# VectorE's written order over more of the input projection and over memory attention, and the residual added by accumulating stores

## The chip, the cores and the metric

The kernel runs on one core of a Trainium2 chip. The metric is the device time of one execution in microseconds: 2166.34 us before, the median of three runs (2165.52 to 2167.77). The profiled execution took 2162.43 us.

The engines are called as in the profile: PE (TensorE, matmul), DVE (VectorE), ACT (ScalarE), POOL (GpSimd) and SP (SyncE, which here only issues DMAs).

## The reference

One residual block of a streaming encoder: 512 tokens, model width 2048, float32.

```
h = rms_norm(x, norm_g)
proj = h @ w_in                      # all branches and gates in one projection
c_gate, b_gate, u, conv_z, c_q, c_kv, k_rope_raw, mla_z, mem_q, mem_z, g_conv, g_mla, g_mem = split(proj)
o_conv = (b_gate * conv3(c_gate * u) * silu(conv_z)) @ w_conv_out
o_mla  = (latent_attention(c_q, c_kv, k_rope_raw) * silu(mla_z)) @ w_mla_out      # 16 heads, chunk-causal
o_mem  = (memory_attention(mem_q, mem) * silu(mem_z)) @ w_mem_out                 # 4 heads of 256 into 256 memory tokens
merged = sigmoid(g_conv) * o_conv + sigmoid(g_mla) * o_mla + sigmoid(g_mem) * o_mem
out = x + merged @ w_o
```

Memory attention normalizes queries and keys, takes softmax over the 256 memory tokens and multiplies by the values.

## The kernel before, in words

**Precision.** Each float32 product is three matmuls of high and low parts (mm3, L161 to L163): whi·xhi, whi·xlo, wlo·xhi. A weight tile is split by ACT, which copies the high part (L281, or L154 for plain tiles), and then by DVE, which subtracts it to get the low part (L282, or L155).

**Panels.** The input projection, the latent attention's output projection (mla_out) and w_o are done by panels of 2x2 blocks with seven products for eight (a Strassen form). Its weights are made by `pair_weights` (L270 to L283) in stages: a DMA into one of four raw buffers (L274, issued by SP), three sums on DVE (L276 to L278), the high part on ACT (L281), the low part on DVE (L282; two buffers each for whi and wlo). A panel has four chunks of 42 matmuls 128x256. After its last chunk the four banks are evicted and combined on DVE (L318 to L327) into a tile e.

**What hands out the stages.** `take()` gives the matmuls of chunk k their weights, and at that point emits whi and wlo of chunk k+1, the sums of k+2 and the load of k+3, and then pops one closure of the list `fills`. So the order of the calls of `take` is the order in which an engine sees these stages, if its order is as written. For PE and SP it always is. For DVE it is inside `tc.manual_schedule(engines={DVE})`; outside, a scheduler with its own estimate of times orders DVE's rows. ACT and POOL are ordered by the scheduler.

**The stages of the program, with their times in the profiled execution.** The memory's keys and values (0 to 106 us); the input projection (106 to 1354), whose first panels run while the transformed input xp is still being made; latent attention by heads, with the gates and memory queries (to 1646); memory attention (1646 to 1692) interleaved with conv_out; the rest of conv_out (to 1735); mla_out (to about 1900); mem_out (to 1984); w_o (1984 to 2156).

**Memory attention** is four generators, one a head, stepped by a string that is written by hand (0 to 3 is a head's next step, w a step of conv_out with three matmuls of 512 columns):

```
ORDER_MEM = "0 0 5w 1 1 5w 0 0 2 2w 1 1 3 2w 0 0 2 2 w 1 1 3 3 2w 2 2 2w 3 3 w 2 2 3 3"
```

The steps of a head (`mem_attend`) are: loads; two steps of scores, each for half of the queries (matmuls, max on DVE L1152, exponentials on ACT L1159, reciprocal of the sums on DVE L1162, scaling of p on ACT L1164); two steps of transposes of p on PE (L363) with the split of the transposed p into high and low parts, pt (ACT L130, DVE L132); two steps of values (matmuls, product with the gate on DVE L1180, split into my by ACT and DVE, store).

**w_o and the residual.** Each of its eight panels loads the residual xr (SP), adds the evicted e to it on DVE (L1350, two rows) and stores both halves by ACT. The last panel has its own tail. The inputs of w_o, xo0 to xo7, are made on the way from the merged branches by `pair_sums` and `pair_split` (`sums_out`, `split_out`).

Of the kernel before, what the change touches and what calls it, by code (L numbers as in the profile page):

```python
# [30 lines left out]
P = 128  # L31
# [76 lines left out]
def body(ctx, tc, a, out):  # L108
# [221 lines left out]
    def panels(xp, weight, n, make, finish, first="acc", tail=None):  # L330

        order = [(0, c) for c in range(3)] + [(1, c) for c in range(3)] + [(0, 3), (1, 3)]
        order += [(i, c) for i in range(2, n) for c in range(4)]
        upcoming(*[pair_job(weight[i][c]) for i, c in order])
        tags = (first, "aux" if first == "acc" else "acc")
        steps, es = {}, {}

        def go():  # L340
            for i, c in order:
                if c == 0:
                    es[i], middle = make(i)
# [179 lines left out]
    def staged_parts():  # L523
# [3 lines left out]
    upcoming(*plain_jobs([a["w_mem_kv"][grp][c] for grp in range(4) for c in range(8)], 512, True,  # L527
                         (staged_parts, None, None),
                         lambda c: memory_load(c + 1) if c < 4 else None))
    work = panels(xp, a["w_h"], len(SEQUENCE), lambda n: make(n), lambda n, e: finish(n, e), "aux")  # L530
    queue.insert(32 + 15, [lambda: rotary_weights()])
    parts_of_x = all_parts()
    manual_dve = ExitStack()
# [48 lines left out]
                nc.scalar.dma_start(mvdram[2 * (grp - 2) + i], t)  # L582
    for _ in parts_of_x:
        pass
    begin(2, 2)
    close_st()
    close_mt()
    pxb, close_xb = open_pool("xb", "right")
# [170 lines left out]

    conv_e = {}  # L760

    def make(n):
        return etile(), None

    angles = rotary()
# [50 lines left out]
    for i in (6, 7):  # L816
# [1 line left out]
        x_load(i, etile())  # L818
        steps = x_pair(i)
        fills += [lambda steps=steps: (next(steps), next(steps)), lambda steps=steps: next(steps)]  # L820
    for _ in range(6):
        next(work)
    manual_dve.close()
    for _ in work:
# [10 lines left out]

    PLACES = ((2, 3), (6, 7), (4, 5), (0, 1))

    def block(n):  # L840
        t = ph.tile([P, 2, S], F32R, tag=f"blk{n // 2}", name="blk", bufs=2)
# [289 lines left out]
    def mem_attend(head):  # L1131
# [9 lines left out]
        nc.sync.dma_start(z, mzdram[head])  # L1141
        yield
        pr = []
        for i2 in range(2):
            sb = bank("aux")
            for ii in range(2):
                cols = slice((2 * i2 + ii) * P, (2 * i2 + ii + 1) * P)
                for f in range(2):
                    mm3(sb[:, ii * M:(ii + 1) * M], (q[:, f, 0, cols], q[:, f, 1, cols]),
                        mk[f], f == 0, f == 1)  # L1150
            mx = pq.tile([P, 2], F32, tag="mx", name="mx", bufs=2)
            vec.tensor_reduce(out=mx, in_=sb.rearrange("p (a b) -> p a b", a=2), op=ALU.max, axis=AX.X)  # L1152
            nm = pq.tile([P, 2], F32, tag="nm", name="nm", bufs=2)
            c0 = 4 * head + 2 * i2
            vec.tensor_tensor(out=nm, in0=mx, in1=mqn[:, c0:c0 + 2], op=ALU.mult)
            sm = pq.tile([P, 2], F32, tag="sm", name="sm", bufs=2)
            p = pq.tile([P, 2, M], F32, tag="p", name="p", bufs=4)
            for ii in range(2):
                act.activation(p[:, ii], sb[:, ii * M:(ii + 1) * M], AF.Exp, scale=mqs[:, c0 + ii:c0 + ii + 1],  # L1159
                               bias=nm[:, ii:ii + 1], accum_out=sm[:, ii:ii + 1])  # L1160
            ri = pq.tile([P, 2], F32, tag="ri", name="ri", bufs=2)
            vec.reciprocal(ri, sm)  # L1162
            for ii in range(2):
                act.activation(p[:, ii], p[:, ii], AF.Copy, scale=ri[:, ii:ii + 1])  # L1164
                pr.append(p[:, ii])
            yield
        pts = []
        for j in range(2):
            b = transpose4([t[:, j * P:(j + 1) * P] for t in pr])
            t = pq.tile([P, 2, S], F32R, tag=f"pt{j}", name=f"pt{j}", bufs=2)  # L1170
            split(b, t[:, 0], t[:, 1])
            pts.append((t[:, 0], t[:, 1]))
            yield
# [12 lines left out]
    m = [mem_attend(head) for head in range(4)]  # L1186
    next(m[0])
    next(m[1])
    run(ORDER_MEM, w=conv, **{str(n): m[n] for n in range(4)})
    close_q()  # L1190
    close_g()
    close_q1()
# [99 lines left out]
    def split_out(n):  # L1292
# [8 lines left out]
                 17: ((split_out, 1), (merged, 2), (merged, 3), (gate_load, 5), (gate_load, 6)),  # L1301
                 22: ((sums_out, 2),), 23: ((split_out, 2),), 24: ((sums_out, 3),),
                 25: ((split_out, 3), (merged, 4), (merged, 5), (gate_load, 7)),
                 29: ((sums_out, 4),), 30: ((split_out, 4), (merged, 6)), 31: ((sums_out, 5),),
                 32: ((split_out, 5),)}

    late_blocks = []
    for k in (6, 7):
# [28 lines left out]

    def make_o(n):
        def middle():
            xrs[n] = pe.tile([P, 2, S], F32, tag="xr", name="xr", bufs=2)  # L1340
            nc.sync.dma_start(xrs[n].rearrange("p f n -> p (f n)"), a["xT"][:, n])
        return pe.tile([P, 8, H], F32, tag="e", name="e", bufs=2), middle

    def finish_o(n, e):
        fills.append(lambda: result(n, e))

    def result(n, e):
        xr = xrs[n]
        for f in range(2):
            vec.tensor_tensor(out=xr[:, f], in0=two(e)[:, f], in1=xr[:, f], op=ALU.add)  # L1350
            nc.scalar.dma_start(out[(2 * n + f) * P:(2 * n + f + 1) * P], xr[:, f])

    def tail_o(b, e):

# [10 lines left out]
        nc.sync.dma_start(out[15 * P:16 * P], xr[:, 1])  # L1365

    merged(7)
    fills += [lambda: None, lambda: sums_out(6), lambda: split_out(6), lambda: sums_out(7), lambda: split_out(7)]
    for n, _ in enumerate(work):
        if n == 8:  # L1370
            manual_dve.close()
# [79 lines left out]
```

## Time and profile before

| what | us |
|---|---|
| median of the runs | 2166.34 |
| profiled execution | 2162.43 |
| its span | 2160.7 |
| PE busy | 2122.6 (98% of the span) |
| DVE busy | 1728.2 (80%) |
| ACT busy | 1010.8 (47%) |

The span is the profiled execution from its first instruction to its last; the execution's own time is 1.7 us longer. A row of the chip's timeline has the start in us, the duration in us, the engine, the line and the operation with its output and inputs, and in brackets the idle time of the engine before it with what ended it. Rows on DVE and ACT overlap at their ends, so that the distance between two starts is a little less than a row's duration: a wlo of 128x1792 lasts 2.02 us, and the next row may start 1.94 after it.

### The profile page before, as it was taken

The numbers are of one execution on the slowest core, as the hardware profiler recorded it, in microseconds if no ns is written. First come the engines' busy times: TensorE is split into PE (matmuls) and PEld (weight loads), VectorE is DVE, ScalarE is ACT, GpSimd is POOL, SyncE is SP. The second block draws the span as 40 slices with busy tenths as digits, with TensorE's granted clock in tenths as the row PEclk, the third lists the DMA queues.
The fourth block names the chain that finished last, engine by engine and source line by source line (L and its number), as shares of the span: only waits on it lengthen the run. The fifth ranks groups of instructions, "written<-read, shape, count | busy, mean of one in ns | idle before, by whom it ended". The sixth has DMA issues, their size and how long they took to land.

```text
span 2160.7 us, 38707 instructions
## 1 busy us (share of the span) xinstructions
PE 2122.6 (98%) x16040; PEld 2037.7 (94%) x16040; DVE 1728.2 (80%) x2740; ACT 1010.8 (47%) x1235; POOL 130.9 (6%) x189
## 2 busy tenths in 40 slices
PE   9989999999999999999999999999999999999899
PEld 7889999999999999999999999898988899987899
DVE  5986878888888888888878876788886688856886
ACT  6743444444444344344444444777765533323333
POOL 0000000000000000000000000212111100011000
PEclk9999999999999999999999999999999999999999
DMA  8634443333333333343444336222346957667443
GB/s 330 248 98 137 158 135 128 128 127 128 127 127 127 125 125 126 126 136 133 137 137 142 131 129 241 90 104 81 112 158 245 355 203 208 201 213 199 141 162 107
DMA packets 93441, 338.51 MB, mean 157 GB/s; under 512 B 10896, under 2 KB 11152, under 8 KB 91216
## 3 DMA queue, kind: packets, MB, share of 16 engines
q1 hardware_dynamic: 70848, 252.58, 34.5%
q0 software_dynamic: 13920, 59.51, 8.6%
q10 hardware_dynamic: 8496, 23.94, 3.1%
q8 instruction: 125, 2.05, 0.4%
q14 instruction: 52, 0.43, 0.1%
HBM read 273.34 MB, written 62.65 MB: 156 GB/s over the span
## 4 chain that ended last, share of the span: by engine, by line
PE 84%; DVE 5%; ACT 2%; DMA 2%; issue 1%; POOL 0%; DVEq 0%; ACTq 0%; POOLq 0%
PE acc L161 14%; PE acc L163 14%; PE acc L162 14%; PE aux L161 13%; PE aux L163 13%; PE aux L162 13%; DVE wlo L282 2%; PE aux L363 1%; PE aux L997 1%; DMA raw<-in_w_h 1%; ACT whi L281 1%; DVE raw L276 0%; PE aux L977 0%; PE aux L980 0%; PE aux L978 0%
## 5 line engine op out<-in xcount | busy, mean ns | idle before, releaser
L281 ACT ACTIVATE whi<-raw 128x1792 fp32r<-128x1792 f32 x304 | 517.6, 1703 | 795.6 <-PE aux L162 336.7
L282 DVE TENSOR_TENSOR wlo<-raw,whi 128x1792 fp32r<-128x1792 f32 x304 | 614.8, 2022 | 204.2 <-ACT whi L281 203.5
L163 PE MATMUL aux<-xp,wlo 128*128 128x256 f32 (+1 forms) x1712 | 479.8, 280 | 6.3 <-DVE wlo L282 6.2
L161 PE MATMUL aux<-xp,whi 128*128 128x256 f32 (+1 forms) x1712 | 480.4, 281 | 0.0
L162 PE MATMUL aux<-xp,whi 128*128 128x256 f32 (+1 forms) x1712 | 479.2, 280 | 0.0
L163 PE MATMUL acc<-xp,wlo 128*128 128x256 f32 x1680 | 470.2, 280 | 3.4 <-DVE wlo L282 3.4
L161 PE MATMUL acc<-xp,whi 128*128 128x256 f32 x1680 | 470.8, 280 | 0.0
L162 PE MATMUL acc<-xp,whi 128*128 128x256 f32 x1680 | 469.6, 280 | 0.0
L163 PEld LDWEIGHTS aux<-xp,wlo 128*128 128x128 f32 (+1 forms) x1712 | 321.1, 188 | 7.5 <-DVE wlo L282 7.5
L161 PEld LDWEIGHTS aux<-xp,whi 128*128 128x128 f32 (+1 forms) x1712 | 320.6, 187 | 0.0
L163 PEld LDWEIGHTS acc<-xp,wlo 128*128 128x128 f32 x1680 | 316.0, 188 | 4.6 <-DVE wlo L282 4.6
L162 PEld LDWEIGHTS aux<-xp,whi 128*128 128x128 f32 (+1 forms) x1712 | 320.2, 187 | 0.0
L161 PEld LDWEIGHTS acc<-xp,whi 128*128 128x128 f32 x1680 | 315.6, 188 | 0.0
L162 PEld LDWEIGHTS acc<-xp,whi 128*128 128x128 f32 x1680 | 315.1, 188 | 0.0
L276 DVE TENSOR_TENSOR raw<-raw 128x512 f32<-128x512 f32 x304 | 208.3, 685 | 36.5 <-DMA raw<-in_w_h 31.8
L155 DVE TENSOR_TENSOR wlo<-raw,whi 128x1024 fp32r<-128x1024 f32 (+2 forms) x89 | 100.5, 1131 | 75.1 <-ACT whi L154 72.7
L154 ACT ACTIVATE whi<-raw 128x1024 fp32r<-128x1024 f32 (+2 forms) x89 | 87.7, 986 | 101.4 <-PE acc L162 43.3
L278 DVE TENSOR_TENSOR raw<-raw 128x256 f32<-128x256 f32 x304 | 127.9, 422 | 6.3
L277 DVE TENSOR_TENSOR raw<-raw 128x256 f32<-128x256 f32 x304 | 127.9, 422 | 5.7
L161 PE MATMUL acc<-whi,blk 128*128 128x384 f32 (+1 forms) x224 | 84.2, 376 | 0.0
L356 POOL TENSOR_TENSOR rs_r<-rs_t,mhalf 128x2 f32<-128x2 f32 (+2 forms) x71 | 65.2, 929 | 276.7 <-DVE rs_t L355 217.2
L163 PE MATMUL acc<-whi,blk 128*128 128x384 f32 (+1 forms) x224 | 80.9, 361 | 0.0
(360 smaller groups left out, 3896.7 us busy)
## 6 DMA issues: line engine op xcount, KB each, us to landing
raw<-in_w_h SPq DMA_DIRECT2D x240, 512.0 KB, 3.5
raw<-in_w_mla_out SPq DMA_DIRECT2D x32, 512.0 KB, 4.2
raw<-in_w_o SPq DMA_DIRECT2D x32, 512.0 KB, 3.6
raw<-in_w_mem_kv SPq DMA_DIRECT2D x31, 512.0 KB, 7.4
gdram<-e ACTq DMA_DIRECT2D x22, 512.0 KB, 2.9
raw<-in_w_ukv SPq DMA_DIRECT2D x16, 512.0 KB, 4.3
raw<-in_w_conv_out SPq DMA_DIRECT2D x16, 512.0 KB, 8.3
aadram<-z POOLq DMA_DIRECT2D x8, 896.0 KB, 3.9
```

The lines of the kernel that those rows point to most:

```text
L154: act.activation(hi[:, cols], raw[:, cols], AF.Copy)
L155: vec.tensor_tensor(out=lo[:, cols], in0=raw[:, cols], in1=r32(hi[:, cols]), op=ALU.subtract)
L161: nc.tensor.matmul(o, lhsT=s[0], rhs=m[0], start=start, stop=False, skip_group_check=shared)
L162: nc.tensor.matmul(o, lhsT=s[0], rhs=m[1], start=False, stop=False, skip_group_check=shared)
L163: nc.tensor.matmul(o, lhsT=s[1], rhs=m[0], start=False, stop=stop, skip_group_check=shared)
L276: vec.tensor_tensor(out=f[:, 4:6], in0=f[:, 1:3], in1=f[:, 0:1].to_broadcast([P, 2, 256]), op=ALU.add)
L277: vec.tensor_tensor(out=f[:, 6], in0=f[:, 5], in1=f[:, 1], op=ALU.add)
L278: vec.tensor_tensor(out=f[:, 7], in0=f[:, 6], in1=f[:, 3], op=ALU.add)
L281: act.activation(hi, f[:, 1:8], AF.Copy)
L282: vec.tensor_tensor(out=lo, in0=f[:, 1:8], in1=r32(hi), op=ALU.subtract)
L356: pool.tensor_tensor(out=r, in0=t, in1=mhalf[:, :n], op=ALU.pow)
L363: nc.tensor.transpose(out=b[:, i * P:(i + 1) * P], in_=s, identity=ident)
```

## The change

Four things are done, all in the program order:

1. DVE's written order covers nine rather than six of the yields of the input projection's loop, the evicted tiles of its first two panels are finished from `fills` rather than at once, and `begin(2, 1)` rather than `begin(2, 2)` starts the queue.
2. Memory attention is put inside `tc.manual_schedule(engines={DVE})`. In `mem_attend` the reciprocal and the scaling become a function `scaled`: the first half of a head's rows is scaled at the end of its second score step, the second half at the beginning of its first transposing step.
3. The residual: seven of the eight blocks of x are copied from DRAM into the output during the panels 12 to 18 of the input projection (SP's queue), and each of w_o's first seven panels is added to it by an accumulating store of POOL. The loads of xr, the additions and ACT's stores go, but for the last panel.
4. `split_out(5)` moves from step 32 of mem_out into `fills`, behind the first chunk's wlo of w_o, and two entries of PLACES, by which tiles take their places, are swapped.

```diff
-    work = panels(xp, a["w_h"], len(SEQUENCE), lambda n: make(n), lambda n, e: finish(n, e), "aux")
+    work = panels(xp, a["w_h"], len(SEQUENCE), lambda n: make(n),
+                  lambda n, e: fills.append(lambda: finish(n, e)) if n < 2 else finish(n, e), "aux")
...
-    begin(2, 2)
+    begin(2, 1)
...
+    def out_rows(n):
+        return out[2 * n * P:2 * (n + 1) * P].rearrange("(f p) n -> p f n", f=2)
+
     def make(n):
+        if n >= 12 and n < 19:
+            nc.sync.dma_start(out_rows(n - 12), a["xT"][:, n - 12].rearrange("p (f n) -> p f n", f=2))
         return etile(), None
...
-    for _ in range(6):
+    for _ in range(9):
         next(work)
     manual_dve.close()
...
-    PLACES = ((2, 3), (6, 7), (4, 5), (0, 1))
+    PLACES = ((2, 3), (4, 5), (6, 7), (0, 1))
...
+        def scaled(p, sm):
+            ri = pq.tile([P, 2], F32, tag="ri", name="ri", bufs=2)
+            vec.reciprocal(ri, sm)
+            for ii in range(2):
+                act.activation(p[:, ii], p[:, ii], AF.Copy, scale=ri[:, ii:ii + 1])
+                pr.append(p[:, ii])
+
+        waiting = []
...
-            ri = pq.tile([P, 2], F32, tag="ri", name="ri", bufs=2)
-            vec.reciprocal(ri, sm)
-            for ii in range(2):
-                act.activation(p[:, ii], p[:, ii], AF.Copy, scale=ri[:, ii:ii + 1])
-                pr.append(p[:, ii])
+            waiting.append((p, sm))
+            if i2 == 1:
+                scaled(*waiting[0])
             yield
         pts = []
         for j in range(2):
+            if j == 0:
+                scaled(*waiting[1])
             b = transpose4([t[:, j * P:(j + 1) * P] for t in pr])
...
-    run(ORDER_MEM, w=conv, **{str(n): m[n] for n in range(4)})
+    with tc.manual_schedule(engines={DVE}):
+        run(ORDER_MEM, w=conv, **{str(n): m[n] for n in range(4)})
...
-                 29: ((sums_out, 4),), 30: ((split_out, 4), (merged, 6)), 31: ((sums_out, 5),),
-                 32: ((split_out, 5),)}
+                 29: ((sums_out, 4),), 30: ((split_out, 4), (merged, 6)), 31: ((sums_out, 5),)}
...
     def finish_o(n, e):
-        fills.append(lambda: result(n, e))
...
+        nc.gpsimd.dma_start(out_rows(n), two(e), accum_op=ALU.add)
...
-    fills += [lambda: None, lambda: sums_out(6), lambda: split_out(6), lambda: sums_out(7), lambda: split_out(7)]
+    fills += [lambda: split_out(5), lambda: sums_out(6), lambda: split_out(6), lambda: sums_out(7), lambda: split_out(7)]
```

How rows move. First DVE in the input projection, from the wlo of the chunk that the prediction calls W5 to that of W8; names with numbers are tiles, raw_1208 being the raw weights of W6, raw_1364 (before) those of a chunk three further on. Before:

```order
L282 TENSOR_TENSOR wlo_1255<-raw_1146,whi_1254 128x1792
L276 TENSOR_TENSOR raw_1208<-raw_1208 128x512
L277 TENSOR_TENSOR raw_1312<-raw_1312 128x256
L277 TENSOR_TENSOR raw_1208<-raw_1208 128x256
L278 TENSOR_TENSOR raw_1312<-raw_1312 128x256
L278 TENSOR_TENSOR raw_1208<-raw_1208 128x256
L276 TENSOR_TENSOR raw_1364<-raw_1364 128x512
L277 TENSOR_TENSOR raw_1364<-raw_1364 128x256
L282 TENSOR_TENSOR wlo_1306<-raw_1208,whi_1305 128x1792
```

and with the change:

```order
L282 TENSOR_TENSOR wlo_1306<-raw_1208,whi_1305 128x1792
...
L282 TENSOR_TENSOR wlo_1357<-raw_1261,whi_1356 128x1792
L276 TENSOR_TENSOR raw_1312<-raw_1312 128x512
L277 TENSOR_TENSOR raw_1312<-raw_1312 128x256
L278 TENSOR_TENSOR raw_1312<-raw_1312 128x256
L318 TENSOR_TENSOR e_1024<-aux_1026,e_1024 128x2x256
L323 TENSOR_TENSOR e_1024<-aux_1027,e_1024 128x512
L276 TENSOR_TENSOR raw_1489<-raw_1489 128x512
L324 SCALAR_TENSOR_TENSOR e_1024<-aux_1027,e_1024 128x256
L326 TENSOR_TENSOR e_1024<-aux_1028,e_1024 128x256
L327 TENSOR_TENSOR e_1024<-aux_1028,e_1024 128x256
L282 TENSOR_TENSOR wlo_1414<-raw_1312,whi_1413 128x1792
```

Between the wlos of W5, W6 and W7 only the chunk's own three sums are left; a sum of a far chunk (raw_1489) and the evictions of a panel now stand between the wlos of W7 and W8.

Second ACT in memory attention, from the exponentials of head 2 (p_18959 and p_18984 before, p_18968 and p_18989 with the change) to the first split of its transposed rows. Before:

```order
L1159 ACTIVATE p_18959,sm_18958<-aux_18941,nm_18956,mqs_98 128x256 x2
L1159 ACTIVATE p_18984,sm_18983<-aux_18966,nm_18981,mqs_98 128x256 x2
L1164 ACTIVATE p_18959<-p_18959,ri_18962 128x256 x2
L130 ACTIVATE my_19002<-mz_18692 128x512
L1164 ACTIVATE p_18984<-p_18984,ri_18987 128x256 x2
L130 ACTIVATE my_19014<-mz_18692 128x512
L1159 ACTIVATE p_19036,sm_19035<-aux_19018,nm_19033,mqs_98 128x256 x2
L1159 ACTIVATE p_19061,sm_19060<-aux_19043,nm_19058,mqs_98 128x256 x2
L130 ACTIVATE pt0_19079<-aux_19074 128x512
```

and with the change:

```order
L1176 ACTIVATE p_18968,sm_18967<-aux_18950,nm_18965,mqs_98 128x256 x2
L1176 ACTIVATE p_18989,sm_18988<-aux_18971,nm_18986,mqs_98 128x256 x2
L1157 ACTIVATE p_18968<-p_18968,ri_18992 128x256 x2
L130 ACTIVATE my_19007<-mz_18699 128x512
L130 ACTIVATE my_19019<-mz_18699 128x512
L1176 ACTIVATE p_19041,sm_19040<-aux_19023,nm_19038,mqs_98 128x256 x2
L1176 ACTIVATE p_19062,sm_19061<-aux_19044,nm_19059,mqs_98 128x256 x2
L1157 ACTIVATE p_19041<-p_19041,ri_19065 128x256 x2
L1157 ACTIVATE p_18989<-p_18989,ri_19075 128x256 x2
L130 ACTIVATE pt0_19084<-aux_19079 128x512
```

The scaling of head 2's second half (p_18984, now p_18989) moved from ahead of head 3's exponentials to behind them and behind head 3's first scaling. On DVE each low part of my now stands directly behind its product, ahead of the max of head 3:

```order
L1197 TENSOR_TENSOR mz_18699<-aux_18999,mz_18699 128x512
L132 TENSOR_TENSOR my_19007<-mz_18699,my_19007 128x512
L1197 TENSOR_TENSOR mz_18699<-aux_19011,mz_18699 128x512
L132 TENSOR_TENSOR my_19019<-mz_18699,my_19019 128x512
L1169 TENSOR_REDUCE mx_19036<-aux_19023 128x2
```

Before, that max stood between the two.

Third DVE in w_o, from the sums ahead of one wlo to the next but one. Before:

```order
L1350 TENSOR_TENSOR xr_21930<-e_21874,xr_21930 128x512 x2
L318 TENSOR_TENSOR e_22040<-aux_22042,e_22040 128x2x256
L323 TENSOR_TENSOR e_22040<-aux_22043,e_22040 128x512
L324 SCALAR_TENSOR_TENSOR e_22040<-aux_22043,e_22040 128x256
L326 TENSOR_TENSOR e_22040<-aux_22044,e_22040 128x256
L327 TENSOR_TENSOR e_22040<-aux_22044,e_22040 128x256
L282 TENSOR_TENSOR wlo_22330<-raw_22213,whi_22329 128x1792
```

and with the change:

```order
L318 TENSOR_TENSOR e_22048<-aux_22050,e_22048 128x2x256
L323 TENSOR_TENSOR e_22048<-aux_22051,e_22048 128x512
L276 TENSOR_TENSOR raw_22392<-raw_22392 128x512
L324 SCALAR_TENSOR_TENSOR e_22048<-aux_22051,e_22048 128x256
L326 TENSOR_TENSOR e_22048<-aux_22052,e_22048 128x256
L327 TENSOR_TENSOR e_22048<-aux_22052,e_22048 128x256
L282 TENSOR_TENSOR wlo_22334<-raw_22219,whi_22333 128x1792
```

The two additions of the residual are gone from between the wlos, and a sum of a far chunk (raw_22392) stands in the evictions. PE's program order is the same in both kernels.

More of the change, by code (lines that the diff above doesn't have):

```diff
@@ L1339, in middle @@
         def middle():
-            xrs[n] = pe.tile([P, 2, S], F32, tag="xr", name="xr", bufs=2)
-            nc.sync.dma_start(xrs[n].rearrange("p f n -> p (f n)"), a["xT"][:, n])
+            if n == 7:
+                xrs[n] = pe.tile([P, 2, S], F32, tag="xr", name="xr", bufs=1)
+                nc.sync.dma_start(xrs[n].rearrange("p f n -> p (f n)"), a["xT"][:, n])
         return pe.tile([P, 8, H], F32, tag="e", name="e", bufs=2), middle
     def finish_o(n, e):
-        fills.append(lambda: result(n, e))
[L1347 to L1351, printed above, removed]
+        nc.gpsimd.dma_start(out_rows(n), two(e), accum_op=ALU.add)
     def tail_o(b, e):
```

## The prediction

> **What bounds the kernel now.** I read the page first, then the busy time by stretches, then what the matrix engine waits for in the stretches that the change touches, then the engines' rows there.
>
> ```profile
> span 2160.7 us, 38707 instructions
> PE 2122.6 (98%) x16040; PEld 2037.7 (94%) x16040; DVE 1728.2 (80%) x2740; ACT 1010.8 (47%) x1235; POOL 130.9 (6%) x189
> ...
> 100.00:200.00 100.00, 90.17 (x711) 87.20 (x710) 82.62 (x112) 43.29 (x38) 2.00 (x5) 0.98 0.40 132
> 200.00:1300.00 1100.00, 1099.16 (x9330) 1098.18 (x9329) 912.24 (x1269) 461.76 (x352) 13.35 (x18) 1.00 0.40 130
> 1646.00:1692.00 46.00, 43.38 (x242) 36.63 (x241) 31.98 (x63) 29.88 (x74) 6.94 (x13) 0.96 0.69 243
> 1692.00:1760.00 68.00, 66.70 (x386) 58.83 (x385) 51.99 (x57) 30.30 (x22) 9.70 (x18) 1.00 0.84 325
> 1960.00:2050.00 90.00, 78.27 (x545) 71.39 (x545) 76.72 (x104) 33.57 (x26) 6.20 (x9) 1.00 0.52 158
> 2050.00:2160.00 110.00, 106.23 (x903) 106.03 (x901) 86.06 (x118) 36.36 (x26) 0.00 (x0) 0.99 0.40 135
> ```
>
> The columns of the stretches are PE, weight loads, DVE, ACT, POOL, granted clock, DMA share, GB/s. PE is the bound: 1099.16 of 1100 us in the long middle. Nothing can be won where it has no gaps. The gaps are at 100–200 (9.8 us), in memory attention (2.6), around 1692–1760 (1.3) and 1960–2050 (11.7). A change that removes no matmul can win only there, and can lose wherever it makes PE wait. Next, what PE waits for, in the windows 100–175, 1646–1692 and 1980–2050:
>
> ```profile
> PE aux L163 <- DVE wlo L282: 5.4, 3, 3.0
> ...
> PE aux L363 <- ACT p L1164: 2.4, 3, 1.7
> ...
> PE acc L163 <- DVE wlo L282: 9.8, 7, 2.6
> ```
>
> The numbers are us in total, times, and the longest. In the first and third stretch it is the low part of the weights (wlo, VectorE), in memory attention the scaled softmax rows (p, ScalarE).
>
> **Part A: VectorE's order in the input projection.** A chunk is 42 matmuls, 4.95 us on PE (1099.16 us for 9330 in the long middle), and every third product needs wlo. In the program order of before, VectorE comes to sums of a far chunk whose raw weights have not landed, ahead of the wlo that PE needs next:
>
> ```profile
> 142.47 0.69 DVE L276 TENSOR_TENSOR raw<-raw 128x512 f32<-128x512 f32 x1 [3.01 <-DMA raw<-in_w_h]
> ...
> 143.54 2.02 DVE L282 TENSOR_TENSOR wlo<-raw,whi 128x1792 fp32r<-128x1792 f32 x1
> ...
> 149.13 0.69 DVE L276 TENSOR_TENSOR raw<-raw 128x512 f32<-128x512 f32 x1 [1.84 <-DMA raw<-in_w_h]
> ...
> 150.20 2.02 DVE L282 TENSOR_TENSOR wlo<-raw,whi 128x1792 fp32r<-128x1792 f32 x1
> ...
> DMA to landing us min/median/max: 3.3/3.5/4.9
> ```
>
> The last row is the landing of the raw loads from 100 to 165 us. The waits of 3.01 and 1.84 are what PE loses at 145.6 and 152.3 (I number the chunks by their wlo: W6 is the one of 143.54, W7 of 150.20). In the new order only the chunk's own sums (0.60 + 0.46 + 0.46, start to start: 1.52) and wlo (1.94) stand there: 3.46 per chunk, below 4.95. So W6 starts its third products at 141.3 rather than 145.6, W7 at 146.7 rather than 152.3: 5.6 us gained. But the written order now puts a far sum ahead of W8. Its load is issued when W7's wlo ends, about 146.7; landing 3.4 gives 150.1, its first sum (0.60) and three evictions (1.02) bring wlo to 151.9, PE to 153.9 instead of 157.3: 3.4 left. Ahead of W9 stand another such sum (loaded from 153.9, landing 4 to 4.9) and ten more rows (5.3 us, partly under the load): PE at about 162.3, as before (162.4). What stays is behind that: the weight load rows of W10 start at 171.6 now, after 0.94 us of waiting for an evicted e at L641, which is then no longer late: 0.9 gained. And the clock:
>
> ```profile
> 170.00:174.00 4.00, 4.00 (x28) 4.00 (x28) 3.62 (x7) 0.93 (x2) 0.47 (x1) 0.71 0.39 131
> 174.00:178.00 4.00, 4.00 (x31) 4.00 (x31) 1.03 (x2) 0.00 (x0) 0.07 (x1) 0.86 0.66 266
> ```
>
> The slow stretch here costs 1.7 us (0.29 x 4 + 0.14 x 4). It may stay or go with the waiting before it; I take half of it. **A = -1.7** (0.9 and 0.85), bounds -2.6 and +1.5 (W8 and W9 each wait for a landing of 4.9). After 200 us PE has no gap to give back, so nothing else there can pay.
>
> **Part B: memory attention.** Here ScalarE and VectorE are the narrow engines:
>
> ```profile
> 1656.18 0.55 ACT L1159 ACTIVATE p<-aux,nm,mqs 128x256 f32<-128x256 f32 x1
> ...
> 1658.86 0.91 ACT L1164 ACTIVATE p<-p,ri 128x256 f32<-128x256 f32 x2
> ...
> 1676.24 0.91 ACT L1164 ACTIVATE p<-p,ri 128x256 f32<-128x256 f32 x2
> 1677.04 0.63 ACT L130 ACTIVATE my<-mz 128x512 fp32r<-128x512 f32 x1
> 1677.56 0.91 ACT L1164 ACTIVATE p<-p,ri 128x256 f32<-128x256 f32 x2
> ...
> 1678.91 0.69 DVE L1152 TENSOR_REDUCE mx<-aux 128x2 f32<-128x512 f32 x1
> ...
> 1680.36 0.57 ACT L1159 ACTIVATE p<-aux,nm,mqs 128x256 f32<-128x256 f32 x1 [1.36 <-PE aux L163]
> ...
> 1661.83 1.17 PE L363 MATMUL aux<-ident,p 128*128 128x128 f32 x6 [1.68 <-ACT p L1164]
> 1664.98 2.05 PE L363 MATMUL aux<-ident,p 128*128 128x128 f32 x8
> 1681.55 1.03 PE L363 MATMUL aux<-ident,p 128*128 128x128 f32 x8
> 1684.87 1.16 PE L363 MATMUL aux<-ident,p 128*128 128x128 f32 x6 [0.56 <-ACT p L1164]
> ```
>
> A head's transposes (L363) need all of its rows scaled. Before, each half was scaled at once (0.80 a pair, start to start); head 2's second half at 1677.56, four microseconds before its transposes at 1681.55, which wait for nothing. Now the second half's scaling stands in the head's transposing step, and on ScalarE that is behind both of head 3's exponentials and its first scaling. Head by head, with the same spacings:
>
> - Head 0: 6.7 us of ScalarE work, two of head 1's exponentials included, lie between 1656.2 and its last scaled row, against 5.9: its last transposes start 0.75 later.
> - Head 1: its second half waits behind two mv halves (0.52 each, as the my row at 1677.04 has it), their low parts on VectorE (0.60 each) and then a reciprocal: its transposes end 1669.05 instead of 1666.8. All together 2.3 late.
> - Head 2: VectorE's low my rows, now written ahead of the max of the next head, wait for ScalarE's high ones (0.52, and 0.60 for a half tile on VectorE, in turn), so the max of head 3 (L1152, 1678.91) comes at 1683.3 where a shift of 2.3 alone would give 1681.2. Two exponentials (1.08 a half) and head 3's first scaling (0.80) end at 1687.3, and head 2's second half is scaled 1687.3 to 1688.1. Its transposes could begin at 1683.8, so PE waits about 4 us.
> - Head 3: its second scaling stands behind head 2's two pt halves and a reciprocal behind their low parts: its last four transposes start at 1691.4. The next conv_out product starts at 1692, against 1685.8.
>
> That is 6.2 to 6.75 late; nothing behind it gives time back, as PE is busy 66.70 of the next 68 us. **B = +6.5**, bounds +3 (the ping-pong of VectorE and ScalarE hidden, only the scaling late: 2.3 + 0.8) and +8.5 (one more half-clock stretch, see rivals).
>
> **Part C: residual.** VectorE loses two additions a panel (L1350), SP seven loads, ScalarE fourteen stores; POOL gets seven accumulating stores.
>
> ```profile
> 1996.12 2.03 DVE L282 TENSOR_TENSOR wlo<-raw,whi 128x1792 fp32r<-128x1792 f32 x1 [1.90 <-ACT whi L281]
> ...
> 2001.57 2.03 DVE L282 TENSOR_TENSOR wlo<-raw,whi 128x1792 fp32r<-128x1792 f32 x1 [0.38 <-ACT whi L281]
> ...
> 2034.45 1.28 DVE L1350 TENSOR_TENSOR xr<-e,xr 128x512 f32<-128x512 f32 x2
> ...
> 2043.43 0.69 DVE L276 TENSOR_TENSOR raw<-raw 128x512 f32<-128x512 f32 x1 [0.53 <-DMA raw<-in_w_o]
> ...
> 2045.30 2.02 DVE L282 TENSOR_TENSOR wlo<-raw,whi 128x1792 fp32r<-128x1792 f32 x1
> ...
> DMA to landing us min/median/max: 3.4/3.6/5.0
> ```
>
> From 1996 on the loop wlo, sums, whi, wlo runs in 5.45 us a chunk, and PE loses 0.4 on each: the additions are not in that loop. Two of them (1.2) stand ahead of the wlo of 2038.16 and two (1.2) ahead of that of 2045.30. Moving split_out(5) behind the first wlo of w_o brings that one 1.15 earlier. Against it, far sums now stand ahead of the next wlo in their place, and these wait for loads: with a landing of 3.5 us 2.1 is won by 2047, with 4.5 0.1, with 5.0 0.9 lost (the last row is the landing from 1985 to 2050). The load of 5.0 was issued at 1992.7, right behind an accumulating store:
>
> ```profile
> L1287 POOL DMA_DIRECT2D mgdram<-gt x8: 852/876/882, 1917.3 to 1991.1; - x8
> ```
>
> There will be one such store a panel, so I take 4.4. **C = -0.3**, bounds -2.1 and +0.9. After 2050 PE has no wait to lose, so the other five panels' additions are worth nothing.
>
> **Part D: what I cost at nothing.** The seven copies of the residual into the output, about 345 to 465 us, share the queues with raw loads, and SP issues them among these:
>
> ```profile
> 353.35 0.69 DVE L276 TENSOR_TENSOR raw<-raw 128x512 f32<-128x512 f32 x1
> ...
> 363.14 0.69 DVE L276 TENSOR_TENSOR raw<-raw 128x512 f32<-128x512 f32 x1
> ```
>
> A load issued as the wlo before 353.35 frees its buffer is first read at 363.14: 9.8 us for a landing of 3.5 as between 100 and 165, 6 of cover; a copy as long as one or two such landings in front fits. Without cover: about 1 us each (4.9 less 3.5 is 1.4 at most), 7 in all. The swapped PLACES only swap buffers: 0.
>
> **The sum** is -1.7 + 6.5 - 0.3 = +4.5. The profiled execution took 2162.43 (span 2160.7 and 1.7 around it), the median is 2166.34; the profiled one would be 2166.9, and the median **2170.8** (+0.21%).
>
> **Rivals.**
> 1. Written order pays (faster). If the scaled rows of the second half are not what the transposes end up waiting for, because ScalarE has 16 of 46 us free there, memory attention sheds its 2.4 us of waits and part of the 1.6 of slow clock; A at -2.6 and C at -2.1: 2166.3 - 2.4 - 2.6 - 2.1 = 2159.2. Against it: ScalarE is full just there (4.00 of 4 us in both rows under 3). It decides when p of head 2 is scaled before 1682.5.
> 2. B is only half (no change): 2.3 + 0.8, then -1.7 - 0.3: 2167.4. It speaks for this that ScalarE and VectorE have more free time around heads 2 and 3 than around 0 and 1; against it, that the written order lets neither run ahead.
> 3. A second slow stretch of the clock. The long idle of head 2 (about 4 us) is followed by half speed, as the short waits of head 0 were:
>
> ```profile
> 1660.00:1664.00 4.00, 2.25 (x11) 1.73 (x11) 1.02 (x3) 4.00 (x14) 0.00 (x0) 0.91 1.01 393
> 1664.00:1668.00 4.00, 4.00 (x16) 2.94 (x16) 2.49 (x4) 4.00 (x9) 0.00 (x0) 0.66 0.19 69
> ```
>
> PE was idle 1.75 of 4 us, and the next four ran at 0.66; about 1.7 us lost (0.09 x 4 + 0.34 x 4). Once more: 2172.5. The Trainium skill (TensorE: Matmul & The Clock Gate, Part 1: The HAM clock gate) has the array at half rate after an idle window of some 3.4 us that runs free of the program. By that rule the 4 us of head 2 bring the stretch only if they cover a window; this trace is less strict, since 1.75 us idle were enough at 1663.
> 4. The copies or the accumulating stores hold up raw loads (7 x 1 us): 2177.8. For it: the load that landed in 5.0 beside an accumulating store; against: 6 us of cover.
>
> **How the numbers follow.** Forecast 0.40, rival 2 0.30, rival 3 0.10, rival 4 0.05, rival 1 0.15. A difference below 0.2% (4.3 us) can't be told from none here. Faster: rival 1, 0.15. Slower: rivals 3 and 4 and 0.32 of the forecast's 0.40, since its centre lies just over the bound: 0.47. No change: rival 2 and the other 0.08, 0.38. Signs are mixed, so the likeliest case's own range is 2167.5 to 2174; the whole is 2161 to 2176.
>
> **What would show it.** A: no wait for a DMA ahead of the wlos at 143 and 150, but one ahead of W8 and W9; W10 at 170–171. B: ScalarE's scaling of head 2's second half behind head 3's exponentials, and PE's wait before the third transpose of head 2 near 4 us; no such wait makes the forecast wrong. C: the losses around 2032–2047 as large as before. D: no PE wait between 345 and 470.

## The result and the profile after

The changed kernel takes 2181.36 us (median of four, 2180.22 to 2182.47), the kernel before 2165.93 beside it: a ratio of 1.0076, 95% interval 1.0063 to 1.0089. The change makes the kernel 15.4 us slower. The forecast was 2170.8, the stated range ended at 2176. The sign was right; two thirds of the size were missing.

The page of the profiled execution after:

```profile
span 2180.4 us, 38663 instructions
PE 2132.5 (98%) x16040; PEld 2047.6 (94%) x16040; DVE 1721.2 (79%) x2726; ACT 1012.2 (46%) x1235; POOL 139.5 (6%) x196
```

Its busy time by stretches (columns as before: PE, weight loads, DVE, ACT, POOL, granted clock, DMA share, GB/s; the stages come up to 20 us later than before, so the stretches are moved along):

```profile
100.00:200.00 100.00, 92.81 (x718) 89.52 (x716) 84.31 (x113) 44.26 (x38) 2.05 (x5) 0.97 0.40 133
1644.00:1698.00 54.00, 43.14 (x231) 36.94 (x230) 27.38 (x57) 29.45 (x71) 5.17 (x10) 0.91 0.52 188
1974.00:2070.00 96.00, 83.61 (x556) 77.49 (x555) 75.94 (x103) 33.42 (x26) 8.62 (x11) 0.95 0.51 136
2070.00:2180.00 110.00, 105.66 (x898) 105.45 (x896) 79.70 (x105) 36.36 (x26) 5.88 (x5) 0.99 0.42 112
```

PE is idle 10.9 us in memory attention, where it was 2.6, and the granted clock there is 0.91 rather than 0.96. Around w_o it fell from 1.00 to 0.95. PE is busy 9.9 us longer on the same matmuls: that is the slower clock.

What PE waits for, from 1644 to 1698 and from 1996 to 2070 (us in total, times, longest):

```profile
PE aux L363 <- ACT p L1157: 10.7, 3, 4.0
...
PE acc L163 <- DVE wlo L282: 11.1, 5, 4.9
```

Before these read 2.4 and 9.8.

PE's order is the same in both kernels, so the two traces can be laid beside each other matmul by matmul. The table has the excess of each start over the usual distance for that width (118 ns for 256 columns), by the stage in which the matmul stood before. The first number is the waits, the second the stretches at slow clock, which are runs of matmuls at about twice the distance:

| us lost by PE | 106–200 | 1645–1693 | 1693–1760 | 1760–1960 | 1960–2030 | 2030–2053 | slow in all |
|---|---|---|---|---|---|---|---|
| before | 11.8 + 1.6 | 5.0 + 1.2 | 1.7 + 0 | 0 + 0 | 7.9 + 0 | 7.0 + 0 | 4.2 |
| the change | 9.6 + 3.0 | 13.4 + 3.4 | 4.1 + 1.4 | 2.0 + 0 | 4.6 + 1.5 | 10.2 + 2.8 | 13.6 |
| without memory attention's part | 12.1 + 2.8 | 4.9 + 1.1 | 2.1 + 0 | 0 + 0 | 4.2 + 1.5 | 7.5 + 3.0 | 10.8 |
| that part alone | 11.3 + 1.5 | 13.3 + 3.7 | 4.1 + 0 | 0 + 0 | 7.5 + 0 | 6.1 + 1.5 | 8.6 |
| the residual alone | 13.1 + 2.8 | 4.9 + 1.2 | 1.8 + 0 | 0 + 0 | 6.7 + 0 | 7.6 + 3.1 | 8.6 |

Over the whole span the waits grew by 10.1 us (47.7 to 57.8) and the slow stretches by 9.4: half and half of the 19.7 us between the two spans. The profiled execution before had a high clock (0.998, where the executions of that kernel have 0.993 to 0.998, their median at 0.996), so that the medians lie less far apart than the traces. The changed kernel has 0.991 to 0.994 in all four. About 0.3% of 2170, some 7 us, is therefore the clock of the kernel and not of one execution.

### The profile page after: what moved, and what is told of

Read it like the earlier page. It is cut to its first block, busy times and chain, and to the rows that moved or that the text cites. A ratio compares the mean times of both kernels' runs of the same rounds, so it can differ in the third digit from the quotient of the medians.

```text
span 2180.4 us, 38663 instructions
## 1 busy us (share of the span) xinstructions
PE 2132.5 (98%) x16040; PEld 2047.6 (94%) x16040; DVE 1721.2 (79%) x2726; ACT 1012.2 (46%) x1235; POOL 139.5 (6%) x196
## 4 chain that ended last, share of the span: by engine, by line
PE 79%; issue 7%; DVE 7%; DMA 4%; ACT 2%; POOL 0%; SPq 0%; ACTq 0%; DVEq 0%; POOLq 0%
PE acc L163 14%; PE acc L162 14%; PE acc L161 14%; PE aux L163 11%; PE aux L162 11%; PE aux L161 11%; DVE wlo L282 2%; DMA mgdram<-gt 1%; PE aux L1005 1%; DVE raw L276 1%; ACT whi L281 1%; DMA mgdram<-sg 1%; DMA raw<-in_w_o 1%; PE aux L363 1%; PE aux L985 0%
```

## The experiments

### The parts taken apart

The first four kernels undo or keep whole parts. Without memory attention's part (`mem_attend` is as before too, with reciprocal and scaling at the end of each score step):

```diff
-    with tc.manual_schedule(engines={DVE}):
-        run(ORDER_MEM, ...)
+    run(ORDER_MEM, ...)
...
```

> The change without its part in memory attention (VectorE there left to the scheduler, each half scaled at once); projection order, residual and split_out(5) as changed. Theory: memory attention's part (10.8 us up to 1693) also causes what is lost after it up to 1840 (4.6 us, gate loads and my stores that come later), so both go and +2 to +4 us is left: -1.3 at the start, +3 to +5 in w_o; time about 2169, and PE's waits at wlo between 1735 and 1840 are those of before. Rival: the losses of 1746 to 1840 come from elsewhere (swapped places, or the output copies): they stay, about 2173.

Measured: 2166.51 us, ratio 1.0015 (1.0006 to 1.0025). The waits of 1645 to 1840 are those of before, as the theory has it: the losses in that stretch need memory attention's part, and the swapped places and the copies don't bring them.

That part alone, on the kernel before:

> The kernel before with the change's part in memory attention alone. Theory: +11 us up to 1693 and +4 to +5 more up to 1840, nothing in w_o: about 2181. Rival: only the 11 us, 2177. If the half-speed stretches are chance and not brought by the waits, less by up to 4 us, 2173 to 2177.

Measured: 2177.49, ratio 1.0063 (1.0046 to 1.0080). Its 11 us up to 1693 are there again (8.3 of waits and 2.5 of clock) and 2.4 behind it. The 2.0 us that the changed kernel lost between 1760 and 1960 are neither here nor in the kernel without that part. They lie behind a raw load that landed in 7.1 us; whether they belong to that one execution or to the parts together, and what made the load late, stays open.

The residual alone (copies, accumulating stores, no additions; `split_out(5)` where it was):

```diff
+        if n >= 12 and n < 19:
+            nc.sync.dma_start(out_rows(n - 12), a["xT"][:, n - 12]...)
-        fills.append(lambda: result(n, e))
+        nc.gpsimd.dma_start(out_rows(n), two(e), accum_op=ALU.add)
```

> The kernel before with the residual's part alone (copies, accumulating stores, no additions; split_out(5) where it was). Theory: raw loads issued beside an accumulating store land in 6 to 6.5 us, not 3.5, and the sums that wait for them stand ahead of the next wlo: +5 us in w_o around 2030 to 2050, nothing at 340 to 490: about 2171. Rival: without the moved split_out(5) PE is later there and the landing is hidden: 2166 to 2167.

Measured: 2168.58, ratio 1.0021 (1.0011 to 1.0030). That is 4.5 us slower, about as much as expected, but not in the expected way: in its trace PE loses only 2.5 us more than before between 1960 and 2053, and these are slow stretches (3.1), while the waits there are 0.6 shorter. Another 2.5 are lost ahead of 200 us, where this kernel's text is that of before. The copies cost PE nothing, as the stretch of the changed kernel where they run shows:

```profile
340.00:500.00 160.00, 160.00 (x1361) 160.00 (x1361) 135.20 (x183) 65.88 (x51) 1.06 (x2) 1.00 0.45 149
```

PE is busy 160 of 160 us, with the DMA share up from 0.39 to 0.45.

The projection's order, the places and the moved `split_out(5)` without the other two parts:

> The kernel before with the projection's order, the swapped places and the moved split_out(5) alone. Theory: -1.3 us by 200 and -2 at the first chunks of w_o, kept as the residual's additions stay: about 2163. Rival: the 2 us of w_o are given back at its second panel, 2165.

Measured: 2161.17, ratio 0.9990 (0.9978 to 1.0003), so not told from no change. The parts add up: -0.10, +0.21 and +0.63% are 0.74, against 0.76 for the whole.

### Which half of memory attention's part

VectorE's written order alone, each half scaled at once as before:

```diff
-    run(ORDER_MEM, w=conv, **{str(n): m[n] for n in range(4)})
+    with tc.manual_schedule(engines={DVE}):
+        run(ORDER_MEM, w=conv, **{str(n): m[n] for n in range(4)})
```

> The kernel before with VectorE's written order in memory attention alone; each half is scaled at once, as before. Theory: the late scaling is what the transposes of heads 0, 1 and 2 wait for (it stands behind the next head's exponentials on ScalarE), so most of the 11 us are not there: +2 to +5, 2166 to 2169, and PE has no 4 us wait before head 2's transposes. Rival: the written order makes VectorE and ScalarE wait for each other in turn (my high and low), and scaling at once only moves the wait: +8 to +12 as with both.

Measured: 2171.41, ratio 1.0037 (1.0022 to 1.0051). And the late scaling alone, with VectorE left to the scheduler:

> The kernel before with the late scaling alone; VectorE in memory attention left to the scheduler. Theory: head 2's second half is scaled behind head 3's exponentials also here, 3 to 4 us of wait at its transposes, 1 to 2 at heads 0 and 1: +5 to +9, 2169 to 2172. Rival (the written order is the cause): within 2 us of before.

Measured: 2168.00, ratio 1.0014 (1.0002 to 1.0027). My theory, that the late scaling is most of it, is wrong: by the traces the written order alone costs 7.4 us between 1645 and 1693, the late scaling alone 3.4, and together they cost 10.8, their sum. PE's waits at the transposes with the written order alone:

```profile
PE aux L363 <- ACT p L1164: 6.8, 5, 1.8
```

and with the late scaling alone:

```profile
PE aux L363 <- ACT p L1149: 6.1, 3, 3.6
```

There are five short ones in the first (at heads 0, 1 and 3) and three in the second, one of them long. A reason for the short ones stands in VectorE's rows of the first kernel, here for head 3:

```profile
1691.01 0.17 DVE L1162 RECIPROCAL ri<-sm 128x2 f32<-128x2 f32 x1 [1.27 <-ACT p L1159]
1691.09 0.67 DVE L1152 TENSOR_REDUCE mx<-aux 128x2 f32<-128x512 f32 x1
```

The reciprocal of a head's first half is written ahead of the max of its second, and waits 1.27 us for the first half's exponentials; so the second half's exponentials start that much later: the two max rows of head 3 are 2.2 us apart there (1688.86 and 1691.09), and PE waits 1.5 for the second half's rows. In the changed kernel, where the late scaling moves that reciprocal, they are 0.8 apart (1685.28 and 1686.07), and head 3's transposes wait for nothing. The late scaling thus takes one wait of the written order away and brings its own. Head 2's max rows are as far apart with the written order alone, but its transposes don't wait: a late row counts only where PE comes to it first.

### The ping-pong of VectorE and ScalarE

In the written order each product mz is followed by its own split into my, whose low part needs ScalarE's high part. ScalarE's rows for head 0 in the changed kernel:

```profile
1674.79 0.63 ACT L130 ACTIVATE my<-mz 128x512 fp32r<-128x512 f32 x1 [4.91 <-DVE mz L1197]
1676.79 0.63 ACT L130 ACTIVATE my<-mz 128x512 fp32r<-128x512 f32 x1 [1.36 <-DVE mz L1197]
```

and with the late scaling alone:

```profile
1674.26 0.63 ACT L130 ACTIVATE my<-mz 128x512 fp32r<-128x512 f32 x1 [2.28 <-DVE mz L1189]
1675.42 0.63 ACT L130 ACTIVATE my<-mz 128x512 fp32r<-128x512 f32 x1 [0.52 <-DVE mz L1189]
```

The two stand 2.00 us apart in the one and 1.16 in the other. The next kernel keeps memory attention as changed and puts both products ahead of both splits:

```diff
             vec.tensor_tensor(out=z[:, f], in0=yb, in1=z[:, f], op=ALU.mult)
-            t = pq.tile([P, 2, S], F32R, tag="my", name="my", bufs=4)
-            split(z[:, f], t[:, 0], t[:, 1])
-            nc.gpsimd.dma_start(amdram[2 * head + f], r32(t))
+            for g in range(2) if f == 1 else ():
+                t = pq.tile([P, 2, S], F32R, tag="my", name="my", bufs=4)
+                split(z[:, g], t[:, 0], t[:, 1])
+                nc.gpsimd.dma_start(amdram[2 * head + g], r32(t))
```

> Memory attention as changed and the rest as before, but with both products of a head (mz) ahead of both splits into my, so that VectorE doesn't wait for ScalarE between them. Theory: in the written order a my comes 2.0 us after the other where it was 1.2 to 1.4; the max of heads 2 and 3 then comes 1.3 us earlier each, and the gate load behind the last my rows earlier too: 3 to 5 us less than with memory attention as changed, 2172 to 2175. Rival: what counts is the late scaling, and the time stays at 2177.

Measured: 2173.61, ratio 1.0043 (1.0028 to 1.0059), against 1.0063 with memory attention as changed: 4 us less by the medians, as expected, though the two intervals overlap. In its trace the two my rows are 1.37 apart, PE's wait at head 2's transposes fell from 4.0 to 2.5, and the waits behind memory attention from 4.1 to 2.3. Between 1645 and 1693 the trace gains less than its waits say, since its slow stretches grew: PE loses 16.4 us there in all, against 17.0.

```profile
1680.60 0.63 ACT L130 ACTIVATE my<-mz 128x512 fp32r<-128x512 f32 x1 [4.45 <-DVE mz L1189]
1681.97 0.63 ACT L130 ACTIVATE my<-mz 128x512 fp32r<-128x512 f32 x1 [0.74 <-DVE mz L1189]
...
1694.47 1.16 PE L363 MATMUL aux<-ident,p 128*128 128x128 f32 x6 [2.48 <-ACT p L1149]
```

### What the accumulating stores cost

As the change without memory attention's part, with stores that don't accumulate. What this kernel leaves out is the residual of the first seven panels, so that its time is that of plain stores and no more:

```diff
-        nc.gpsimd.dma_start(out_rows(n), two(e), accum_op=ALU.add)
+        nc.gpsimd.dma_start(out_rows(n), two(e))
```

> As the change without memory attention's part, but the stores of w_o's first seven panels don't accumulate, so that the output lacks the residual there. Theory: the raw loads issued beside an accumulating store land in 5.5 to 6.2 us because the store moves its 512 KB twice; with plain stores they land in 3.5 to 4.5, and 2 to 5 us of w_o come back: 2161 to 2164. Rival: any store of POOL's queue slows them as much, and the time stays at 2166.

Measured: 2161.51, ratio 0.9984 (0.9973 to 0.9995), where the same kernel with accumulating stores had 1.0015 (1.0006 to 1.0025): 0.31%, 6.7 us by the ratios (5.0 by the medians, which were not taken side by side). Raw loads from issue to landing in 2015 to 2060, with accumulating stores:

```profile
DMA to landing us min/median/max: 3.4/3.7/6.0
```

and without accumulation:

```profile
DMA to landing us min/median/max: 3.3/3.5/3.9
```

The first raw load behind each store, issued some 1.7 to 2.1 us later, landed in 5.3 to 6.5 us in the four kernels with accumulating stores (the changed one and three of the runs here, 23 loads), and in 3.5 to 4.2 with plain ones (6 loads). It is the accumulation that lengthens the landing, not the queue or the 512 KB. In the traces of the two kernels with and without accumulation, PE's waits from 1960 on are 11.7 with it and 12.5 without, and the slow stretches 4.5 against 1.1: 2.6 us of difference, near the lower end of what the intervals allow (2.4 to 11), and it lies in the slow stretches, not in the waits. So the traces show 2.6 us for the accumulation; the rest of the 6.7 they don't show. The two traces are 6.4 us apart, but 2.3 of these lie between 200 and 1645, where the two texts are the same: in the faster one matmuls of 256 columns ran at 113.3 ns rather than 117.8 for a longer time (from about 1049 to 1166 us against 1052 to 1123), and why is open.

With the accumulating stores as they are, but the written order of w_o kept for 12 chunks:

```diff
-        if n == 8:
+        if n == 12:
             manual_dve.close()
```

> As the change without memory attention's part, with VectorE's written order in w_o kept for 12 rather than 8 chunks: accumulating stores as they are, but no sum of a far chunk ahead of the next wlo up to there. Theory: the long landing costs only as the far sums stand ahead of the wlo; now the loads have a chunk's time more, the waits of 2 to 2.7 us at chunks 8 to 10 shrink to under 1 each and 3 to 5 us come back: 2162 to 2164. Rival: the chunk's own sums now wait for the same landing, or the far sums only move to chunk 12: 2166.

Measured: 2168.22, ratio 1.0025 (1.0011 to 1.0038). The waits of 2030 to 2053 fell from 7.5 to 3.0, as the theory has it, and 7.6 of waits and 3.6 of slow clock appeared behind 2053. The rival is right: the far sums moved on to the twelfth chunk, and there they wait for the next accumulating stores' landings:

```profile
2051.43 0.69 DVE L276 TENSOR_TENSOR raw<-raw 128x512 f32<-128x512 f32 x1 [3.13 <-DMA raw<-in_w_o]
...
2067.71 0.69 DVE L276 TENSOR_TENSOR raw<-raw 128x512 f32<-128x512 f32 x1 [4.08 <-DMA raw<-in_w_o]
```

### Whether more written order gains more

The projection's part with 14 yields rather than 9 (`for _ in range(14)`), so that no far sum stands ahead of W8 and W9:

> The kernel before with the moved split_out(5), the swapped places and VectorE's written order kept for 14 yields of the input projection rather than 9: no far sum stands ahead of the wlos that the prediction calls W8 and W9. Theory: these two waits (2.1 and 1.7 to 2.2 us with 9) shrink to under 1 each, so that 200 us is reached 3 to 4 us earlier than before instead of 1.3, and w_o keeps its 2: 2160 against 2164 of before. Rival: VectorE's evictions and the norm's rows there are the bound, and the same us are lost at W8 to W12 or at the later end of the written order: 2163.

Measured: 2164.48, ratio 1.0007 (0.9997 to 1.0017). W8's wait shrank to 0.9, W9's stayed at 2.2, and PE loses 3.9 at 189 us, where the written order now ends:

```profile
188.97 0.39 PE L163 MATMUL acc<-xp,wlo 128*128 128x256 f32 x1 [3.73 <-DVE wlo L282]
```

The rival again: the loss moves to the end of the written order. The same kernel with the written order of w_o ended after 2 chunks:

```diff
-        if n == 8:
+        if n == 2:
             manual_dve.close()
```

> As the projection with 14 yields, but VectorE's written order in w_o ends after 2 chunks, not 8. Theory: in written order sums, whi and wlo follow each other in 5.45 us a chunk and PE loses 0.4 on each of six chunks, and the change back costs 7 us once, wherever it lies: about 2 us less, 2158 to 2160. Rival: with the transformed inputs still being made the change back is dearer there: 2161 or more.

Measured: 2168.09, ratio 1.0025 (1.0013 to 1.0037). The theory is wrong: nothing is gained. In its trace w_o loses 14.5 us, most of it now in the first panel, against 15.0 with 8 chunks; its trace is 3.3 us longer than that with 8 chunks, but it loses 5.9 more ahead of 1645, where the two texts are the same. So the 3.6 us between the medians are not shown to come from this edit.

The kernel that was left as a candidate, the projection's order with the moved `split_out(5)`, once more:

> The candidate: the kernel before with the projection's order (9 yields), the swapped places and the moved split_out(5), without memory attention's and the residual's parts; once more with more rounds, since its first interval (0.9978 to 1.0003) leaves open whether it beats before. Theory: 1 to 3 us less than before, ratio 0.9985 to 0.9995. Rival: the us gained at 100 to 200 and at the first chunks of w_o are within what the clock takes and gives from run to run, ratio 1.000.

Measured: 2158.83, ratio 0.9982 (0.9961 to 1.0003). Twice 0.1 to 0.2% faster and twice not clear of no change; no version here that keeps the residual is shown to beat the kernel before. The second interval is wide; one of the eleven executions took 2139.99 us, 18 below the next, and what made it so fast is not known.

## Why the prediction was right or wrong

By the table the changed kernel's trace loses 19.8 us more than that of before: -0.8 in the input projection (forecast -1.7), +10.6 in memory attention and +3.8 right behind it (forecast +6.5 for both), +2.0 in mla_out (forecast nothing) and +4.2 in w_o (forecast -0.3). Nearly half of it, 9.4, is the slow clock, for which the sum had a saving of 0.85 and no cost.

**Part A was right step by step, but not in its end.** VectorE's rows of the changed kernel:

```profile
139.50 2.03 DVE L282 TENSOR_TENSOR wlo<-raw,whi 128x1792 fp32r<-128x1792 f32 x1 [1.90 <-ACT whi L281]
144.96 2.02 DVE L282 TENSOR_TENSOR wlo<-raw,whi 128x1792 fp32r<-128x1792 f32 x1 [1.90 <-ACT whi L281]
150.50 0.69 DVE L276 TENSOR_TENSOR raw<-raw 128x512 f32<-128x512 f32 x1 [0.60 <-DMA raw<-in_w_h]
152.10 2.01 DVE L282 TENSOR_TENSOR wlo<-raw,whi 128x1792 fp32r<-128x1792 f32 x1
160.44 2.01 DVE L282 TENSOR_TENSOR wlo<-raw,whi 128x1792 fp32r<-128x1792 f32 x1
```

PE's third products of W6 to W9 start at 141.6, 147.0, 154.2 and 162.5; the forecast had 141.3, 146.7, 153.9 and 162.3. L641 no longer waits. At 173 us PE is 1.3 ahead of the kernel before, at 176 0.8 (forecast 1.7). The clock part failed: I took half of the slow stretch at about 172 as saved, as if waits had brought it. One is there, between 169 and 180 us, in all fourteen traces, and in the eight with a longer written order in the projection PE is busy all through the 3.4 us before it; what brings it stays open. And a wait that the prediction itself had, that for W8, is followed by one more, at 154 to 158:

```profile
154.00:158.00 4.00, 3.83 (x19) 3.83 (x20) 4.00 (x10) 2.13 (x2) 0.30 (x1) 0.57 0.41 135
```

That the table shows only 0.8 of gain is in part the luck of the one trace of before: six traces with this order lose 12.2 to 14.9 us between 106 and 200, six with the order of before 12.8 to 15.9, on the mean 1.4 more.

**Part B: right place, too small.** PE's transposes after:

```profile
1661.52 1.17 PE L363 MATMUL aux<-ident,p 128*128 128x128 f32 x6 [3.50 <-ACT p L1157]
1667.51 1.73 PE L363 MATMUL aux<-ident,p 128*128 128x128 f32 x6 [3.21 <-ACT p L1157]
1690.19 1.73 PE L363 MATMUL aux<-ident,p 128*128 128x128 f32 x6 [4.00 <-ACT p L1157]
1694.16 1.04 PE L363 MATMUL aux<-ident,p 128*128 128x128 f32 x8
```

Head 2's wait of about 4 us is there as forecast, behind ScalarE's scaling as described, and head 3 no longer waits. The bound for late scaling alone was 3.1, and it costs 3.4; the written order, which the forecast had at the other 3.4, costs 7.4 alone. Three steps failed:

- Heads 0 and 1 were mis-sized: 3.5 and 3.2 us of wait, where before there were 1.7 and none. I had 2.3 for both together; laid beside each other, PE goes from 1.5 ahead to 2.0 behind over them, 3.5. ScalarE scales four rows in one go, head 1's first half ahead of head 0's second:

```profile
1660.17 1.69 ACT L1157 ACTIVATE p<-p,ri 128x256 f32<-128x256 f32 x4
```

- The clock inside memory attention was left out of the sum and made a rival at 1.7 and a chance of 0.10. It came, at two places behind waits, and cost 2.2 to 2.5 more than before in both kernels that have this part:

```profile
1667.00:1671.00 4.00, 3.49 (x11) 2.89 (x12) 1.78 (x4) 2.06 (x4) 0.00 (x0) 0.50 0.00 2
1671.00:1675.00 4.00, 4.00 (x13) 3.16 (x13) 2.09 (x3) 0.21 (x1) 0.00 (x0) 0.68 0.00 0
...
1692.00:1696.00 4.00, 4.00 (x19) 3.26 (x19) 1.76 (x4) 2.66 (x6) 0.00 (x0) 0.75 0.16 64
```

- "Nothing behind it gives time back" was put, but not what is late next: VectorE ends memory attention's my rows and evictions later than PE needs, and the next eviction waits for a gate's load:

```profile
1722.52 1.29 DVE L1069 TENSOR_TENSOR sb<-acc,sb 128x512 f32<-128x512 f32 x2 [2.74 <-DMA sb<-gdram]
```

The transformed inputs and the wlos of mla_out come later too, and PE loses 2.4 more between 1693 and 1760, also with that part alone. The gate's load is not shown to be the cause: with both products first, an eviction still waits 2.1 us for it, and the loss is down to 2.3. The order of the my rows is part of it; the rest stays open.

The Trainium skill's rule on the clock gate (TensorE: Matmul & The Clock Gate, Part 1: The HAM clock gate) has the array at half rate after an idle window of some 3.4 us. The slow stretches here last about 3.4 us (2066.1 to 2069.5) or twice that (1666.7 to 1673.5), as that window has it. But idle times shorter than a window were enough: that of 1666.7 began when PE had waited for 2.4 us, and that of 1663 in the kernel before followed 1.75 us; the measurement decides.

The traces give a rule of their own. The stretches start at multiples of 3.41 us from each other. With the time from 110 to 2140 us of all fourteen traces cut at these points, each of the 45 pieces in which PE was idle for 1.9 us or more was followed by a slow one, and 9 of the 20 with 1.7 to 1.9. So a wait's place on that grid counts beside its length: head 0's wait of 3.5 us in the changed kernel fell into two pieces with 1.85 and 1.72 us of idle time and brought nothing; head 1's of 3.2 put 2.4 into one and brought a slow stretch.

**Part C: wrong sign.** I had -0.3 from a landing of 4.4 us, with 5.0 as the worst row. Two steps failed: this landing, and the clock, which was not in C at all. In waits alone C came out at -0.1 (14.8 us against 14.9), with 3.2 more from 2030 on; the slow stretches add 4.3, 2.8 of it behind those longer waits. In the changed kernel two raw loads issued 1.7 us behind an accumulating store landed in 6.5 and 6.1 us, and two sums wait for them ahead of a wlo:

```profile
2052.41 0.69 DVE L276 TENSOR_TENSOR raw<-raw 128x512 f32<-128x512 f32 x1 [3.20 <-DMA raw<-in_w_o]
...
2062.15 0.69 DVE L276 TENSOR_TENSOR raw<-raw 128x512 f32<-128x512 f32 x1 [4.18 <-DMA raw<-in_w_o]
```

The accumulating stores themselves, in the list of transfers (KB each, median us to landing):

```profile
out<-e POOLq DMA_DIRECT2D x7, 512.0 KB, 6.2
```

That far sums would stand there was in the prediction; their price was bounded by one load of the trace (5.0), and a single row is no upper bound for a kind of transfer that the change itself adds. The gain of the moved `split_out(5)` was right: between 1985 and 2005 PE gains 1.1 us in the changed kernel and 1.2 in each of six others that have this move, and nothing in the five without it; the prediction had 1.15. After 2053 the five other panels' stores cost PE nothing (at most 0.3 of excess where w_o's written order is as it was): by then the sums are done a chunk ahead.

**Part D was right:** the copies cost nothing. Rival 4 (copies or stores hold up the raw loads) had the right resource for the stores, with a chance of 0.05 only. The range was too narrow above because three terms that move the same way (waits, the clock that follows waits, what is late next) were each left at their likeliest value. Even the three upper bounds together, +1.5, +8.5 and +0.9, gave no more than 2177.2, and the stated range had left out two of the prediction's own rivals, at 2159.2 and 2177.8.

## What to carry to other kernels

Writing an engine's order by hand fixes the waits that the program's text has: before freezing it, look in the text for a row that needs another engine's answer and put independent rows between (here both products ahead of both splits gave back 4 of 14 us by the medians, with intervals that overlap). Where a written order ends, the loss moves to that place, as it did in two kernels here. Beside every new wait of the matrix engine of some 2 us or more, put the price of a slow stretch of its clock (some 1.5 us here) into the sum; beside every accumulating store, a longer landing for the loads that follow it.

## What the runs showed of the hardware that was not expected

An accumulating store of 512 KB takes 6.2 us to land in the median, a plain one 3.3, and it lengthens the first load of 512 KB issued 1.7 to 2.1 us later to 5.3–6.5 us; behind the same store without accumulation that load takes 3.5 to 4.2. Idle time of 1.9 us or more within one piece of the 3.41 us grid was followed by half speed every time (45 of 45). And the clock's loss per execution (some 4 us in the quietest trace, 8 to 16 in the others) is as large as most of the effects studied here: the changed kernel's mean granted clock was 0.991 to 0.994, that of before 0.993 to 0.998.
